# Full-height products, grouped head outputs and line-aligned operands in a two-block transformer kernel

## The chip, the cores and the metric

The kernel runs on one core of a Trainium2 chip as one program of some 24,000 instructions. The metric is the device time of one execution in microseconds (us). The engines are named as in the profile: PE is TensorE's matrix multiply and PEld its weight load, DVE is VectorE, ACT is ScalarE, POOL is GpSimd, SP is SyncE, which here only starts transfers.

## The reference

Two transformer blocks on 512 tokens of width 1024. The first block has a state space branch (a scan in chunks, 8 groups of 4 heads of 64, state 128, 16 extra tokens in front), a short convolution branch, and a retrieval layer that picks experts by top-k; the second block has two kinds of attention and an MLP. What the change touches is the scan:

```
def step(state, inp):
    xc, ac, bc, cc = inp
    acum = jnp.cumsum(ac, axis=1)
    seg = acum[:, :, None] - acum[:, None, :]
    decay = jnp.exp(jnp.where(causal, seg, -jnp.inf))
    cb = jnp.einsum('blgn,bsgn->blsg', cc, bc)
    y_diag = jnp.einsum('blsgr,bsgrp->blgrp', cb[..., None] * decay, xc)
    y_off = jnp.einsum('blgn,bgrpn->blgrp', cc, state) * jnp.exp(acum)[..., None]
    to_end = jnp.exp(acum[:, -1:] - acum)
    new_state = (state * jnp.exp(acum[:, -1])[..., None, None]
                 + jnp.einsum('blgn,blgr,blgrp->bgrpn', bc, to_end, xc))
    return new_state, y_diag + y_off
...
y = group_rmsnorm(y * jax.nn.silu(z), norm_g, SSD_N_GROUPS)
```

The kernel takes chunks of 128 tokens for the 512, and one of 16 in front.

## The kernel before

**Exact products in three parts.** Nearly every large product is float32 made of three products of a shorter float type: `split` (L170) makes a high part `h` on ACT and a low part `l` on DVE or POOL (`wh`, `wl` of a weight tile `wr`; `uh`, `ul` of the input), and `mm3` (L201) issues, for each of 8 slices of depth, high by high, high by low and low by high. The products that use plain float32 (the scan's own) come in the trace as two instructions each, transposes as one. In `A.matmul(out, s, m)` the second operand is held in the array and has up to 128 columns, the third is streamed and has up to 512.

**A projection** loads a 512 KB weight tile on SP's queue into one of 3 buffers (`weights`, L183), splits it (3 buffers for `wh` and `wl`), and runs either 24 products of 512 columns (`mm3_real`, the 512 real tokens) or 48 of 264 or 258 (`mm3_all`, with the tokens in front, in two halves).

**The state space stage** (`ssd_group`, L554, called for 8 groups) has, for each group: projections `BT`, `CT`, `xT0`, `xT1`, each followed by a convolution of four taps and a silu (`conv_silu`: one ACT pass, three DVE passes, a tanh, one DVE pass); the table `cb` of 128 by 128 for each chunk (product `pcb`); for each of 4 heads a product `pb` that spreads the running sum `acum` over the partitions. Its operands `identr` and `acT` have 64 rows: 32 of high parts, 32 of low parts. From `pb` come `E = exp(pb)` on ACT and the decay `W`: on DVE four instructions of 128 columns, `min(pb - acum of the key's token, 0)`, then one exp of 512 columns on ACT, then a product with `cb` on DVE. POOL multiplies `E` by `CT` in place. Then the loop over chunks: transposes into `ptt`, `xdt` and `xe` (DVE), `bt` (ACT), the product `pst`, the new state `st`. For the first chunk `n` is 16, and transposes, `xe`, `bt` and `pst` have 16 rows. Then for j in 0, 1 the projection `z` of 512 columns, and in `py` the heads' outputs: for each of 4 chunks 4 products with 64 held columns, two heads side by side in halves of the array. `ssd_norm` (L656) is a generator: the first `next` makes the sum of squares (`pq`) and the reciprocal root by Newton steps on DVE (`gqx`, `gqa`, `gqy`); the second spreads it with `pr` and multiplies. Of the next group, both `next` calls stand between its projections.

**What sets the order.** The tile framework's scheduler lays each engine's instructions out in a fixed order when the program is built; an engine then takes them strictly in that order. `keep_in_program_order` and `after` (L831, an edge without a wait) pin single instructions. Buffers come from stacks of memory, one from the left and one from the right (`side="right"`); a tile that is not a multiple of 128 bytes moves the start of all that are opened after it on its side. The right-hand stack starts 96 bytes past a multiple of 128.

**The expert stage** (`up`, `second_mm`, L1060) runs 128 expert blocks: products `psu` of 384 columns, and `acc`, 18 products of 512 columns for a block, whose held operand is `ch` or `cl` and whose streamed one is a `pv` weight tile. While it runs, a gather of 128 rows at a time goes on through POOL's queue and DVE.

Of the kernel before, what the change touches and what calls it, by code (L numbers as in the profile page):

```python
# [9 lines left out]
F32 = mybir.dt.float32  # L10
# [12 lines left out]
S = 512  # L23
NM = 16
# [130 lines left out]
class K:  # L155
# [46 lines left out]
    def mm3(self, ps, w, xs, first=True, last=True):  # L202

        kn = len(xs)
        n, tot = 0, 3 * kn
        wh, wl = w
        for k in range(kn):
            xh, xl = xs[k]
            for a, b in ((wh, xh), (wh, xl), (wl, xh)):
                self.nc.tensor.matmul(ps, a[:, k], b, start=first and n == 0, stop=last and n == tot - 1)  # L210
                n += 1

    def mm3_all(self, ps2, w, x, skip=0):

        xh, xl = [a[:, :, skip:] for a in x]
        H = (T - skip) // 2
        for c in range(2):
            self.mm3(ps2[:, 512 - H + c * H:512 + c * H], w,
                     [(xh[:, k, c * H:(c + 1) * H], xl[:, k, c * H:(c + 1) * H]) for k in range(8)])

# [58 lines left out]
    def run(self):  # L279
        nc = self.nc  # L280
        self.cms = {}
        cp = self.open("const")
        self.wraw = self.open("wraw", 3)
        self.whl = self.open("whl", 3)
        self.pt = cp.tile([128, _PN], F32, name="pt")
        self.ct = cp.tile([128, _CN], F32, name="ct")
        self.ones = cp.tile([128, 128], F32, name="ones")
        nc.vector.memset(self.ones, 1.0)

        nc.scalar.activation(self.ones[:, :1], self.ones[:, :1], AF.Copy)  # L290
        nc.scalar.dma_start(self.pt, self.A["par"])
        self.identr = cp.tile([64, 32], F32R, name="identr")
        self.hp = cp.tile([128, 160], F32, name="hp")
        self.res = cp.tile([128, 8, S], F32, name="res")
        self.g12 = cp.tile([128, 8], F32, name="g12")
        self.dpool = self.open("dram", space=DRAM)
        self.sgd = self.dpool.tile([8, 128, S], F32, name="sgd")
        self.gd = self.dpool.tile([16, 128, S], F32, name="gd")
        self.md = self.dpool.tile([16, 128, NC, 128], F32, name="md")
        self.actd = [self.dpool.tile([128, 8, ND], F32, name="actd%d" % g) for g in range(16)]  # L300
        self.mixers()
        self.peer()
        self.block2()
        self.close(*reversed(list(self.cms)))


    def mixers(self):
# [4 lines left out]
        self.u = [up.tile([128, 8, T], F32R, name=n) for n in ("uh", "ul")]  # L312
# [62 lines left out]
        v.tensor_tensor(self.identr, self.cst("ident")[:64, :32], self.cst("ident")[:64, 32:64], op=OP.add)  # L375
# [94 lines left out]
    def proj_real(self, w, i):  # L470
        ps = self.mmtile()[:, :S]
        self.mm3_real(ps, self.weights(self.A[w][i]), self.u)
        return ps
# [15 lines left out]
    def dt_stage(self, dp, p, v):  # L489
# [30 lines left out]
        ahl = dp.tile([64, T], F32R, name="acumhl")  # L520
        nc.scalar.activation(ahl, ac, AF.Copy)
        nc.vector.tensor_tensor(ahl[32:], ac[32:], ahl[32:].bitcast(F32), op=OP.subtract)
# [3 lines left out]
    def dt_tokens(self, dp, srcs):  # L526
# [8 lines left out]
        v4 = pt[:, :480].rearrange("p (c j h) -> p c j h", c=5, j=3)  # L535
        nc.vector.tensor_copy(tok[:NM, 0], v4[:NM, 0])
        nc.vector.tensor_copy(tok[:, 1:], v4[:, 1:])
        self.tok = tok

# [14 lines left out]
    def ssd_group(self, g, yn, sb, s1):  # L554
# [4 lines left out]
        def proj(w, blk, name, skip=0):  # L559
            ps = self.mmtile()  # L560
            self.mm3_all(ps, self.weights(w), self.u, skip)
# [4 lines left out]
        BT = proj(A["w_b"][g], 16 + g, "BT")  # L566
        CT = proj(A["w_c"][g], 24 + g, "CT", SKIP)
# [3 lines left out]
        next(self.fin, None)  # L571
        xT.append(proj(A["w_x"][2 * g + 1], 2 * g + 1, "xT1"))
# [14 lines left out]
        for h in range(4):  # L587
            hh = g * 4 + h
            pb = sp.tile([128, 512], F32, tag="pa", name="pb")
            nc.tensor.matmul(pb, self.identr[:, hh:hh + 1].to_broadcast([64, 128]), acT[:, NM:],  # L590
                             start=True, stop=True)
            nc.scalar.activation(E[:, h], pb, AF.Exp)
            for c in range(4):
                nc.vector.tensor_scalar(W[:, h, c * 128:(c + 1) * 128], pb[:, c * 128:(c + 1) * 128],
                                        tok[:, c + 1, 0, hh:hh + 1], 0.0, op0=OP.subtract, op1=OP.min)
            nc.scalar.activation(W[:, h], W[:, h], AF.Exp)
# [7 lines left out]
        for c, (o, n) in enumerate(self.chunks):  # L604
# [18 lines left out]
            nc.tensor.matmul(pst, bt[:n], xe[:n], start=True, stop=True)  # L623
# [11 lines left out]
        for j in range(2):  # L635
            pz = self.proj_real("w_z", 2 * g + j)
# [3 lines left out]
            py = sp.tile([128, 512], F32, tag="py", name="py")  # L640

            for c in range(4):
                cs = slice(c * 128, (c + 1) * 128)
                for n, (a, b) in enumerate(((xdt[:, c], W), (states[c], Cx))):
                    for h in (2 * j, 2 * j + 1):
                        r = 64 * (h % 2)
                        nc.tensor.matmul(py[r:r + 64, cs], a[:, h * 64:(h + 1) * 64], b[:, h, cs],
                                         start=n == 0, stop=n == 1, skip_group_check=True)
# [418 lines left out]
    def peer_v(self, mm):  # L1067
# [58 lines left out]
        x, y, a = [rp.tile([128, 2, 4], F32, name=n) for n in ("nrx", "nry", "nra")]  # L1126
# [68 lines left out]
    def block2(self):  # L1195
# [14 lines left out]
        sk8 = qp.tile([128, 8], F32, name="sk8")  # L1210
# [94 lines left out]
        eps4 = cn.tile([128, 4], F32, name="eps4")  # L1305
# [322 lines left out]
```

## Time and profile before

| | us |
|---|---|
| median of 3 runs | 2778.41 |
| lowest, highest | 2777.58, 2779.73 |
| the profiled execution | 2778.32 |
| its span, first to last instruction | 2776.6 |
| state space stage, one group (table `cb` to the next table) | 48.70 |

The profile is one execution. A busy share says how much of the time an engine had an instruction in it. A PE product is recorded from its start to the end of its way through the array, so that products overlap in the records; how long it holds the array is read from one start to the next. The granted clock (PEclk) is TensorE's, as a share of 2.4 GHz.

### The profile page before, as it was taken

How to read it: one execution, taken by the hardware profiler on the slowest of the kernel's cores; microseconds unless marked ns; L12 is line 12 of the kernel's file. 1: busy time of each engine (PE TensorE's matmuls, PEld its weight loads, DVE VectorE, ACT ScalarE, POOL GpSimd, SP SyncE). 2: the span in 40 equal slices, each digit the busy share in tenths (PEclk: the TensorE clock that was granted, in tenths of full speed). 3: DMA queues.
4: the chain of work that ended last, by engine and by line, in shares of the span. 5: the costliest groups of instructions: out<-in, count | busy, mean ns of one | idle time of the engine just before them, and what ended most of it. 6: DMA issues, size and time to landing. Idle time of an engine off the chain costs nothing.

```text
span 2776.6 us, 40120 instructions
## 1 busy us (share of the span) xinstructions
PE 2729.3 (98%) x15546; PEld 2366.1 (85%) x15546; DVE 1905.5 (69%) x3707; ACT 1084.8 (39%) x1730; POOL 725.9 (26%) x406
## 2 busy tenths in 40 slices
PE   8999999999999999999999999999999999999998
PEld 8988888887878999999899898877788777988887
DVE  8433777775259999768887777888887766741225
ACT  4323334344233344444333333333344554543232
POOL 2444445443543002000222221222210000144441
PEclk9999999999999999999999999999999999999999
DMA  4222121223342468889988887999952324333232
GB/s 144 92 95 96 62 66 64 69 66 118 114 144 77 138 235 282 262 291 289 366 323 310 318 307 295 384 367 376 375 191 88 96 83 141 129 107 99 91 99 99
DMA packets 173439, 509.96 MB, mean 184 GB/s; under 512 B 14016, under 2 KB 75456, under 8 KB 156736
## 3 DMA queue, kind: packets, MB, share of 16 engines
q1 hardware_dynamic: 89600, 324.42, 34.1%
q0 software_dynamic: 18432, 134.23, 12.5%
q10 hardware_dynamic: 65216, 48.75, 5.5%
q8 instruction: 122, 2.00, 0.3%
q14 instruction: 69, 0.57, 0.1%
HBM read 457.73 MB, written 49.09 MB: 183 GB/s over the span
## 4 chain that ended last, share of the span: by engine, by line
PE 59%; DVE 12%; DMA 4%; ACT 1%; issue 1%; ACTq 0%; SPq 0%; DVEq 0%
PE psu L210 14%; PE acc L1064 14%; PE mmt L210 6%; PE psup L210 6%; PE psdn L210 6%; PE ps L210 4%; DMA wr<-pv 3%; DVE wl L177 2%; PE psw L210 2%; PE po L210 2%; PE pm L1021 1%; ACT wh L176 1%; PE psml L1582 1%; DVE ae L1007 1%; DVE si L713 1%
## 5 line engine op out<-in xcount | busy, mean ns | idle before, releaser
L176 ACT ACTIVATE wh<-wr 128x1024 fp32r<-128x1024 f32 (+1 forms) x503 | 530.6, 1056 | 1083.5 <-issue 225.1
L177 POOL TENSOR_TENSOR wl<-wr,wh 128x1024 fp32r<-128x1024 f32 x180 | 437.2, 2429 | 947.9 <-ACT wh L176 937.5
L177 DVE TENSOR_TENSOR wl<-wr,wh 128x1024 fp32r<-128x1024 f32 (+1 forms) x323 | 391.6, 1213 | 167.9 <-ACT wh L176 165.8
L869 POOL DMA_INDIRECT gb<-puv,idx x128 | 200.8, 1569 | 928.5 <-DVE gacc L877 775.3
L210 PE MATMUL psu<-u2h,wh 128*128 128x384 f32 x1024 | 347.8, 340 | 0.0
L210 PE MATMUL psu<-u2h,wl 128*128 128x384 f32 x1024 | 344.6, 337 | 0.2 <-DVE wl L177 0.2
L210 PE MATMUL psu<-u2l,wh 128*128 128x384 f32 x1024 | 344.0, 336 | 0.0
L210 PE MATMUL mmt<-uh,wh 128*128 128x264 f32 (+2 forms) x1016 | 327.2, 322 | 0.9 <-DVE sc L486 0.9
L210 PE MATMUL mmt<-ul,wh 128*128 128x264 f32 (+2 forms) x1016 | 327.6, 322 | 0.0
L210 PE MATMUL mmt<-uh,wl 128*128 128x264 f32 (+2 forms) x1016 | 325.1, 320 | 0.0
L1064 PE MATMUL acc<-wh,ch 128*128 128x512 f32 x768 | 306.2, 399 | 4.2 <-ACT ch L176 2.2
L1064 PE MATMUL acc<-wl,ch 128*128 128x512 f32 x768 | 305.7, 398 | 1.3 <-DVE wl L177 1.3
L1064 PE MATMUL acc<-wh,cl 128*128 128x512 f32 x768 | 305.9, 398 | 0.1
L210 PEld LDWEIGHTS mmt<-ul,wh 128*128 128x128 f32 x1016 | 191.3, 188 | 21.3 <-issue 10.0
L210 PEld LDWEIGHTS mmt<-uh,wh 128*128 128x128 f32 x1016 | 191.3, 188 | 15.3 <-issue 1.4
L210 PEld LDWEIGHTS mmt<-uh,wl 128*128 128x128 f32 x1016 | 191.5, 188 | 14.8 <-issue 3.3
L210 PEld LDWEIGHTS psu<-u2h,wh 128*128 128x128 f32 x1024 | 193.6, 189 | 2.2
L210 PEld LDWEIGHTS psu<-u2l,wh 128*128 128x128 f32 x1024 | 193.7, 189 | 2.0
L210 PEld LDWEIGHTS psu<-u2h,wl 128*128 128x128 f32 x1024 | 193.3, 189 | 0.6 <-DVE wl L177 0.6
L1064 PEld LDWEIGHTS acc<-wl,ch 128*128 128x128 f32 x768 | 145.5, 189 | 39.0 <-DVE wl L177 3.5
L1064 PEld LDWEIGHTS acc<-wh,ch 128*128 128x128 f32 x768 | 145.2, 189 | 38.2 <-ACT wh L176 2.9
L1064 PEld LDWEIGHTS acc<-wh,cl 128*128 128x128 f32 x768 | 145.3, 189 | 33.4 <-DVE cl L177 0.4
(515 smaller groups left out, 5448.1 us busy)
## 6 DMA issues: line engine op xcount, KB each, us to landing
wr<-pu SPq DMA_DIRECT2D x128, 512.0 KB, 5.5
wr<-pv SPq DMA_DIRECT2D x128, 512.0 KB, 6.1
mg<-md SPq DMA_DIRECT2D x34, 768.0 KB, 10.1
md<-stg ACTq DMA_DIRECT2D x24, 1024.0 KB, 7.7
wr<-w_dn SPq DMA_DIRECT2D x36, 512.0 KB, 3.7
wr<-w_up SPq DMA_DIRECT2D x35, 512.0 KB, 3.7
actd<-at ACTq DMA_DIRECT2D x79, 192.0 KB, 4.0
ag<-actd SPq DMA_DIRECT2D x19, 768.0 KB, 6.8
```

The source lines that it names most:

```text
L176: nc.scalar.activation(h, src, AF.Copy)
L177: (eng or nc.vector).tensor_tensor(l, src, h.bitcast(F32), op=OP.subtract)
L210: self.nc.tensor.matmul(ps, a[:, k], b, start=first and n == 0, stop=last and n == tot - 1)
L713: v.max_index(x[:, 8:16], m[:, 8:16], s2)
L869: keep(nc.gpsimd.indirect_dma_start(out=rows[k][:NG], out_offset=None, in_=self.A["puv"], in_offset=bass.IndirectOffsetOnAxis(ap=idx[:NG, ...
L1007: v.tensor_tensor(pairs(ae), io.rearrange("p (k r) -> p k r", r=2)[:, None].to_broadcast(B4o), w(iT), op=OP.is_equal)
L1021: nc.tensor.matmul(pm[:, t], ae[:, t, 0], B[:, t, j], start=j == 0, stop=j == 1)
L1064: self.nc.tensor.matmul(self.accs[i], a[:, t], b[:, d], start=e == self.e1 and n == 0, stop=e == self.e1 - 1 and n == 2)
L1582: nc.tensor.matmul(ps[:, :N], qh[:, h, bs], kh[:, h, :N], start=True, stop=True)
```

## The change

Six edits.

1. `identr` and `acT` get 128 rows (64 of them zeros) instead of 64, and the first chunk is treated with 128 rows; the rows of `tok` beyond 16 are zeroed.
2. The products of `py` are chained by `after`: of j = 0 none stands ahead of the last `pst`, of j = 1 none ahead of the last product of its `z`.
3. The low parts `wl` of `BT`, `CT` and the two `z` move from POOL to DVE, four of the six in a group (`xT0`, `xT1` stay on POOL).
4. The decay: one DVE instruction of 512 columns takes `min(pb, acum of the key's token)`; the subtraction becomes the bias of the exp, which is now four ACT instructions of 128 columns. The bias is a new tile `ntok`.
5. The second `next(self.fin)`, with `pr`, moves from before `xT1` to the middle of it.
6. Memory: `u`'s rows are 544 floats of which the view takes the last 528, so that the real tokens start at a multiple of 128 bytes in each row; the small tiles `nrx`, `nry`, `nra` (96 bytes together) become one at the bottom of the right-hand stack; `sk8` and `eps4` are padded. By the addresses in the built program: the held `ch`, `cl` of the expert stage and the streamed `ch`, `cl`, `mh`, `ml` go from 96 bytes past a multiple of 128 to 0; `fh`, `fl`, `oh2`, `ol2`, `m2h`, `m2l` (second block) from 64 to 0; the 512 real columns of `uh`, `ul` from 0 or 64, by row, to 0. The halves of 264 and 258 columns stay off.

```diff
+        nr = self.open("nr", side="right").tile([128, 3, 2, 4], F32, name="nr")
+        self.nr = [nr[:, i] for i in range(3)]
...
-        self.u = [up.tile([128, 8, T], F32R, name=n) for n in ("uh", "ul")]
+        self.u = [up.tile([128, 8, 32 + S], F32R, name=n)[:, :, 32 - NM:] for n in ("uh", "ul")]
...
-        ahl = dp.tile([64, T], F32R, name="acumhl")
-        nc.scalar.activation(ahl, ac, AF.Copy)
-        nc.vector.tensor_tensor(ahl[32:], ac[32:], ahl[32:].bitcast(F32), op=OP.subtract)
+        ahl = dp.tile([128, T], F32R, name="acumhl")
+        nc.gpsimd.memset(ahl[64:].bitcast(F32), 0.0)
+        nc.scalar.activation(ahl[:64], ac, AF.Copy)
+        nc.vector.tensor_tensor(ahl[32:64], ac[32:], ahl[32:64].bitcast(F32), op=OP.subtract)
...
+        nc.gpsimd.memset(tok[:, 0], 0.0)
         nc.vector.tensor_copy(tok[:NM, 0], v4[:NM, 0])
         nc.vector.tensor_copy(tok[:, 1:], v4[:, 1:])
         self.tok = tok
+        self.ntok = dp.tile([128, 4, 32], F32, name="ntok")
+        nc.gpsimd.tensor_scalar(self.ntok, tok[:, 1:, 0], -1.0, None, op0=OP.mult)
...
-        BT = proj(A["w_b"][g], 16 + g, "BT")
-        CT = proj(A["w_c"][g], 24 + g, "CT", SKIP)
+        BT = proj(A["w_b"][g], 16 + g, "BT", eng=nc.vector)
+        CT = proj(A["w_c"][g], 24 + g, "CT", SKIP, eng=nc.vector)
 
         next(self.fin, None)
         xT = [proj(A["w_x"][2 * g], 2 * g, "xT0")]
-        next(self.fin, None)
-        xT.append(proj(A["w_x"][2 * g + 1], 2 * g + 1, "xT1"))
+        xT.append(proj(A["w_x"][2 * g + 1], 2 * g + 1, "xT1", mid=lambda: next(self.fin, None)))
...
-            nc.tensor.matmul(pb, self.identr[:, hh:hh + 1].to_broadcast([64, 128]), acT[:, NM:],
+            nc.tensor.matmul(pb, self.identr[:, hh:hh + 1].to_broadcast([128, 128]), acT[:, NM:],
                              start=True, stop=True)
             nc.scalar.activation(E[:, h], pb, AF.Exp)
+            nc.vector.tensor_tensor(W[:, h].rearrange("p (c l) -> p c l", c=4), pb.rearrange("p (c l) -> p c l", c=4),
+                                    tok[:, 1:, 0, hh:hh + 1].to_broadcast([128, 4, 128]), op=OP.min)
             for c in range(4):
-                nc.vector.tensor_scalar(W[:, h, c * 128:(c + 1) * 128], pb[:, c * 128:(c + 1) * 128],
-                                        tok[:, c + 1, 0, hh:hh + 1], 0.0, op0=OP.subtract, op1=OP.min)
-            nc.scalar.activation(W[:, h], W[:, h], AF.Exp)
+                cs = slice(c * 128, (c + 1) * 128)
+                nc.scalar.activation(W[:, h, cs], W[:, h, cs], AF.Exp, bias=self.ntok[:, c, hh:hh + 1])
...
-        for c, (o, n) in enumerate(self.chunks):
+        for c, (o, _) in enumerate(self.chunks):
+            n = 128
...
-            pz = self.proj_real("w_z", 2 * g + j)
+            pz = self.proj_real("w_z", 2 * g + j, nc.vector)
+            prev = self.last_mm if j else last_st
...
-                        nc.tensor.matmul(py[r:r + 64, cs], a[:, h * 64:(h + 1) * 64], b[:, h, cs],
-                                         start=n == 0, stop=n == 1, skip_group_check=True)
+                        o = nc.tensor.matmul(py[r:r + 64, cs], a[:, h * 64:(h + 1) * 64], b[:, h, cs],
+                                             start=n == 0, stop=n == 1, skip_group_check=True)
+                        self.after(o, prev)
+                        prev = o
...
-        x, y, a = [rp.tile([128, 2, 4], F32, name=n) for n in ("nrx", "nry", "nra")]
+        x, y, a = self.nr
...
-        sk8 = qp.tile([128, 8], F32, name="sk8")
+        sk8 = qp.tile([128, 32], F32, name="sk8")[:, :8]
...
-        eps4 = cn.tile([128, 4], F32, name="eps4")
+        eps4 = cn.tile([128, 16], F32, name="eps4")[:, :4]
```

Outside the state space stage the order on every engine stays as it was, but for `ntok` and the zeroing on POOL. Inside it moves. On PE, at the end of the second group's state loop, before (`mmt` is a projection's product, here the next group's `BT` and `CT`):

```order
L647 MATMUL py_3042<-W_2897,xdt_2943 64x128 x2
L647 MATMUL py_3042<-E_2896,st3_2999 64x128 x2
L210 MATMUL mmt_3116<-uh_98,wh_3119 128x264
L210 MATMUL mmt_3116<-ul_99,wh_3119 128x264
L210 MATMUL mmt_3116<-uh_98,wl_3120 128x264
L210 MATMUL mmt_3116<-uh_98,wh_3119 128x264
L210 MATMUL mmt_3116<-ul_99,wh_3119 128x264
L210 MATMUL mmt_3116<-uh_98,wl_3120 128x264
L210 MATMUL mmt_3180<-uh_98,wh_3183 128x258
L210 MATMUL mmt_3180<-ul_99,wh_3183 128x258
L647 MATMUL py_3042<-W_2897,xdt_2943 64x128 x2
```

and on PE at the same place now:

```order
L638 MATMUL pst_3005<-xe_3003,btok_3001 128x256
L622 MATMUL ptt_3012<-ct_65,xT0_2817 128x128
L622 MATMUL ptt_3012<-ct_65,xT1_2888 128x128
L664 MATMUL py_3050<-W_2905,xdt_2951 64x128 x2
L664 MATMUL py_3050<-E_2904,st0_2962 64x128 x2
L664 MATMUL py_3050<-W_2905,xdt_2951 64x128 x2
L664 MATMUL py_3050<-E_2904,st1_2975 64x128 x2
L664 MATMUL py_3050<-W_2905,xdt_2951 64x128 x2
L664 MATMUL py_3050<-E_2904,st2_2991 64x128 x2
L664 MATMUL py_3050<-W_2905,xdt_2951 64x128 x2
L664 MATMUL py_3050<-E_2904,st3_3007 64x128 x2
```

The four chunks of j = 0 were spread singly among the projections; now they stand in one run behind the last transposes. Over the stage there were 40 runs of `py` products and there are 16.

On DVE, between the second group's table `cb` and the first chunk's `xe`, before (`cacc` and `xT` are the convolution of `xT1`):

```order
L580 TENSOR_TENSOR cb<-pcb,ct 128x512
L549 SCALAR_TENSOR_TENSOR cacc<-mmt,hp,cacc 128x527
L549 SCALAR_TENSOR_TENSOR cacc<-mmt,hp,cacc 128x526
L594 TENSOR_SCALAR W<-pb,tok 128x128
L549 SCALAR_TENSOR_TENSOR cacc<-mmt,hp,cacc 128x525
L594 TENSOR_SCALAR W<-pb,tok 128x128 x3
L552 SCALAR_TENSOR_TENSOR xT_2880<-ctanh,cacc 128x528
L597 TENSOR_TENSOR W<-W,cb 128x512
L594 TENSOR_SCALAR W<-pb,tok 128x128 x4
L620 TENSOR_TENSOR xe<-ptt,tok 16x256
```

and on DVE now, right behind `cb`:

```order
L177 TENSOR_TENSOR wl<-wr,wh 128x1024
L561 SCALAR_TENSOR_TENSOR cacc<-mmt,hp,cacc 128x527
L606 TENSOR_TENSOR W<-pb,tok 128x512
L561 SCALAR_TENSOR_TENSOR cacc<-mmt,hp,cacc 128x526
L561 SCALAR_TENSOR_TENSOR cacc<-mmt,hp,cacc 128x525
L611 TENSOR_TENSOR W<-W,cb 128x512
L606 TENSOR_TENSOR W<-pb,tok 128x512
L564 SCALAR_TENSOR_TENSOR xT_2888<-ctanh,cacc 128x528
L177 TENSOR_TENSOR wl<-wr,wh 128x1024
L611 TENSOR_TENSOR W<-W,cb 128x512
L606 TENSOR_TENSOR W<-pb,tok 128x512
L635 TENSOR_TENSOR xe<-ptt,tok 128x256
```

Two `wl` and the heads' second and third `W` now stand ahead of `xe`, whose product `pst` waits for it. On PE that `pst` moved too, from the 30th to the 40th projection product behind `pcb`.

On PE around `pr`, second group's norm among the third group's projections, before (3269 is `xT0`, 3340 `xT1`):

```order
L210 MATMUL mmt_3269<-uh_98,wh_3272 128x264
L210 MATMUL mmt_3269<-ul_99,wh_3272 128x264
L210 MATMUL mmt_3269<-uh_98,wl_3273 128x264
L258 MATMUL pr_3333<-ct_65,gqy_3255 128x128 x4
L210 MATMUL mmt_3340<-uh_98,wh_3343 128x264
L210 MATMUL mmt_3340<-ul_99,wh_3343 128x264
L210 MATMUL mmt_3340<-uh_98,wl_3344 128x264
```

and on PE there now (3341 is `xT1`):

```order
L210 MATMUL mmt_3341<-uh_102,wh_3344 128x264
L210 MATMUL mmt_3341<-ul_103,wh_3344 128x264
L210 MATMUL mmt_3341<-uh_102,wl_3345 128x264
L260 MATMUL pr_3372<-ct_65,gqy_3263 128x128 x4
L210 MATMUL mmt_3341<-uh_102,wh_3344 128x264
L210 MATMUL mmt_3341<-ul_103,wh_3344 128x264
L210 MATMUL mmt_3341<-uh_102,wl_3345 128x264
```

`pr` now has 24 more products of 264 columns ahead of it.

## Rows read from the trace of the kernel before

**Rows 1.** The page's first part: busy us, share of the span, instructions, by engine.
```profile
PE 2729.3 (98%) x15546; PEld 2366.1 (85%) x15546; DVE 1905.5 (69%) x3707; ACT 1084.8 (39%) x1730; POOL 725.9 (26%) x406
```
**Rows 2.** Windows, one group: stretch, length, busy us (count), clock, DMA share, GB/s.
```profile
319.40:368.10 48.70, 48.27 (x353) 41.15 (x352) 35.44 (x79) 19.32 (x30) 21.86 (x15) 1.00 0.21 67
```
**Rows 3.** Timeline of PE around a 64-row product: start us, us, line, out<-in, shape.
```profile
272.45 0.40 PE L210 MATMUL mmt<-uh,wh 128*128 128x512 f32 x1
...
273.54 0.39 PE L210 MATMUL mmt<-uh,wl 128*128 128x512 f32 x1
```
**Rows 4.** Timeline of PE around the 16-row product of the first chunk.
```profile
280.24 0.49 PE L210 MATMUL mmt<-ul,wh 128*128 128x512 f32 x1
...
281.59 0.48 PE L210 MATMUL mmt<-uh,wl 128*128 128x512 f32 x1
```
**Rows 5.** Timeline of PE around the same products of a later chunk, with 128 rows.
```profile
291.12 0.28 PE L210 MATMUL mmt<-ul,wh 128*128 128x264 f32 x1
...
291.92 0.37 PE L210 MATMUL mmt<-uh,wl 128*128 128x264 f32 x1
```
**Rows 6.** Timeline of PE: one chunk of head outputs between projection products.
```profile
293.22 0.28 PE L210 MATMUL mmt<-uh,wh 128*128 128x264 f32 x1
...
294.24 0.28 PE L210 MATMUL mmt<-uh,wl 128*128 128x264 f32 x1
```
**Rows 7.** Timeline of PE: four chunks of head outputs in one run.
```profile
298.09 0.28 PE L210 MATMUL mmt<-ul,wh 128*128 128x258 f32 x1
...
300.42 0.28 PE L210 MATMUL mmt<-uh,wh 128*128 128x258 f32 x1
```
**Rows 8.** Timeline of PE at the spreading of the norm: in brackets idle time, releaser.
```profile
312.42 0.28 PE L210 MATMUL mmt<-uh,wl 128*128 128x264 f32 x1
313.03 0.65 PE L258 MATMUL pr<-ct,gqy 128*128 128x128 f32 x4 [0.32 <-DVE gqy L253]
```
**Rows 9.** Windows, projections of 512 columns whose operands all start at multiples of 128.
```profile
700.00:740.00 40.00, 40.00 (x178) 33.12 (x177) 2.75 (x4) 0.00 (x0) 1.00 0.37 116
```
**Rows 10.** Windows, L1064: one block's 18 products, held operand 96 past.
```profile
1500.26:1504.47 4.21, 4.21 (x18) 3.20 (x18) 1.00 0.92 346
```
**Rows 11.** Windows, 512 columns: streamed `mh`, `ml` 96 past.
```profile
775.00:800.00 25.00, 25.00 (x109) 20.12 (x108) 3.34 (x5) 0.00 (x0) 1.00 0.50 151
```
**Rows 12.** Windows, 512 columns: streamed `fh`, `fl` 64 past.
```profile
2500.00:2540.00 40.00, 40.00 (x176) 32.81 (x176) 1.00 0.31 99
```
**Rows 13.** Windows: streamed `uh`, `ul`, 512 columns, eight products, 0 or 64 past.
```profile
274.69:276.32 1.63, 1.63 (x8) 1.31 (x7) 1.00 0.58 161
```
**Rows 14.** Windows, 256 columns: sixteen aligned products.
```profile
2445.01:2446.93 1.92, 1.92 (x18) 1.92 (x17) 0.42 (x1) 0.36 (x1) 1.00 0.59 228
```
**Rows 15.** Windows, 256 columns: 20 us with streamed operands 64 past.
```profile
2360.00:2380.00 20.00, 20.00 (x171) 20.00 (x169) 2.61 (x7) 1.00 0.69 215
```
**Rows 16.** Timeline of DVE from the table `cb` to the first chunk's `xe`.
```profile
320.47 0.69 DVE L580 TENSOR_TENSOR cb<-pcb,ct 128x512 f32<-128x512 f32 x1 [1.04 <-PE pcb L577]
...
327.71 0.40 DVE L620 TENSOR_TENSOR xe<-ptt,tok 16x256 f32<-16x256 f32 x1
```
**Rows 17.** Groups of one group's stretch on DVE: line, out<-in, shapes, count, busy us, mean ns.
```profile
L594 DVE TENSOR_SCALAR W<-pb,tok 128x128 f32<-128x128 f32 x16 | 4.6, 340 | 0.7 <-ACT E L592 0.7
L597 DVE TENSOR_TENSOR W<-W,cb 128x512 f32<-128x512 f32 x4 | 4.0, 988 | 0.4 <-ACT W L596 0.4
```
**Rows 18.** The same view on ACT.
```profile
L596 ACT ACTIVATE W<-W 128x512 f32<-128x512 f32 x4 | 2.5, 630 | 3.7 <-DVE W L594 3.6
...
L618 ACT ACTIVATE btok<-ptt 128x128 f32<-128x128 f32 x3 | 0.8, 275 | 3.7 <-DVE xdt L613 3.7
```
**Rows 19.** The page's fifth part: the low parts on DVE.
```profile
L177 DVE TENSOR_TENSOR wl<-wr,wh 128x1024 fp32r<-128x1024 f32 (+1 forms) x323 | 391.6, 1213 | 167.9 <-ACT wh L176 165.8
```
**Rows 20.** Windows, expert stage: PE, PEld, DVE, ACT, POOL, clock, DMA share, GB/s.
```profile
1750.00:1800.00 50.00, 50.00 (x216) 40.17 (x215) 43.14 (x66) 18.00 (x32) 13.09 (x9) 1.00 1.00 400
1900.00:1950.00 50.00, 48.15 (x199) 38.01 (x198) 41.91 (x64) 18.57 (x32) 11.54 (x8) 0.97 0.93 360
```

More of the change, by code (lines that the diff above doesn't have):

```diff
@@ L209, in mm3, with mm3_all @@
             for a, b in ((wh, xh), (wh, xl), (wl, xh)):
-                self.nc.tensor.matmul(ps, a[:, k], b, start=first and n == 0, stop=last and n == tot - 1)
+                self.last_mm = self.nc.tensor.matmul(ps, a[:, k], b, start=first and n == 0, stop=last and n == tot - 1)
                 n += 1
-    def mm3_all(self, ps2, w, x, skip=0):
+    def mm3_all(self, ps2, w, x, skip=0, mid=None):
         xh, xl = [a[:, :, skip:] for a in x]
@@ L219, in mm3_all @@
                      [(xh[:, k, c * H:(c + 1) * H], xl[:, k, c * H:(c + 1) * H]) for k in range(8)])
+            if mid and c == 0:
+                mid()
     def mm3_real(self, ps, w, x, off=NM, n=S):
@@ L291, in run @@
         nc.scalar.dma_start(self.pt, self.A["par"])
-        self.identr = cp.tile([64, 32], F32R, name="identr")
+        self.identr = cp.tile([128, 32], F32R, name="identr")
         self.hp = cp.tile([128, 160], F32, name="hp")
@@ L373, in mixers @@
         sc.append(self.sc_in(sct, 1, d, rb2))
-        v.tensor_tensor(self.identr, self.cst("ident")[:64, :32], self.cst("ident")[:64, 32:64], op=OP.add)
+        v.tensor_tensor(self.identr, self.cst("ident")[:, :32], self.cst("ident")[:, 32:64], op=OP.add)
         o = _POFF["conv_w"][0]
@@ L468, in proj_all, with proj_real @@
         return ps
-    def proj_real(self, w, i):
+    def proj_real(self, w, i, eng=None):
         ps = self.mmtile()[:, :S]
-        self.mm3_real(ps, self.weights(self.A[w][i]), self.u)
+        self.mm3_real(ps, self.weights(self.A[w][i], eng=eng), self.u)
         return ps
@@ L557, in ssd_group, with proj @@
         tok, acT = self.tok, self.acT
-        def proj(w, blk, name, skip=0):
+        def proj(w, blk, name, skip=0, eng=None, mid=None):
             ps = self.mmtile()
-            self.mm3_all(ps, self.weights(w), self.u, skip)
+            self.mm3_all(ps, self.weights(w, eng=eng), self.u, skip, mid)
             o = sb.tile([128, T - skip], F32, tag=name, name=name)
@@ L622, in ssd_group @@
             pst = sp.tile([128, 256], F32, tag="ps", name="pst")
-            nc.tensor.matmul(pst, bt[:n], xe[:n], start=True, stop=True)
+            last_st = nc.tensor.matmul(pst, bt[:n], xe[:n], start=True, stop=True)
             new = s1.tile([128, 256], F32, tag="st%d" % c, name="st%d" % c)
```

## Prediction

> **What bounds the kernel now.** I read the page's first part first: PE is busy for 2729.3 of 2776.6 us, and no other engine passes 69% [rows 1]. That is an average, so next I took the windows view over one group of the state space stage, where most of the change lies: in 48.70 us PE is busy for 48.27, DVE for 35.44, POOL for 21.86, ACT for 19.32, and the granted clock is 1.00 (the 2.4 GHz level) [rows 2]. PE sets the pace there, and DVE has 13 us to spare. A busy PE can still be slow, since records of products overlap. So the third reading is PE's timeline from one start to the next around each kind of product that the change touches [rows 3 to 8], and the fourth the rate of plain projection products by where their operands start [rows 9 to 15]. What the change is worth is what it takes off these starts, less what it makes PE wait for.
>
> **The change part by part.** The sum is made against the profiled execution, 2778.32 us; its span is 2776.6, so 1.7 lie around it. The median of the runs is 2778.41, the same within 0.1.
>
> *The measure: one aligned product of 512 columns.* A window counts products that reach in over its edge: a record lasts 0.39 us [rows 3] and starts come every 0.23, so 1.7 are taken off. With all operands at multiples of 128 bytes that gives 40.00 / (178 − 1.7) = 0.2269 us [rows 9].
>
> *A. `pb` with 128 rows.* From the projection product ahead of a `pb` to the one after the next pass 1.09 us [rows 3]; in it start three products of 512 columns: two of `u` and `pb`. At the 0.2329 of `u`'s products (E below) that would be 0.70. So the 64-row product costs 0.39 us beyond its columns, half at its start, half at the start of what follows. If full height takes this away, 4 × 8 = 32 products give 32 × 0.39 = 12.5 us.
>
> *B. The first chunk with 128 rows.* A projection product, `pst` and the next chunk's three transposes take 1.35 us where `pst` has 16 rows [rows 4], and 0.80 where it has 128, with a projection product of 264 columns (0.12) in place of one of 512 (0.23) [rows 5]; like with like that is 0.80 − 0.12 + 0.23 = 0.91. Eight groups give 8 × 0.44 = 3.5 us. Zeroed rows of `tok` keep the sums the same.
>
> *C. `py` in runs.* One chunk alone takes 1.02 us less two products of 264 columns, 0.78 [rows 6]; four chunks in one run take 2.33 − 0.24 = 2.09, or 0.52 for each [rows 7]. So entering and leaving the half-width products costs about 0.35 us. Per group there were 4 × 0.78 + 2.09 = 5.21 us, and will be 2 × 2.09 = 4.18: 8 × 1.03 = 8.2 us. The chain holds `py` of j = 0 back behind the last transposes; its readers on DVE have all of the second `z` left, so I cost that at nothing, hidden by PE's projections.
>
> *D. `pr` later.* `pr` starts 0.61 us after a product of 264 columns, with 0.32 idle on `gqy` [rows 8]; 0.61 − 0.12 = 0.49, in seven of the eight groups (the last has no projections around it): 3.4 us. Half of `xT1`'s products, 24 × 0.12 = 2.9 us, now lie ahead of it, well over the 0.32. Some 0.1 of the 0.49 may be the products' own start; I take it all.
>
> *E. Alignment.* By one subtraction for each kind: the expert stage's `acc` takes 4.21 / 18 = 0.2339 [rows 10], so 0.0070 over the aligned product, times 128 × 18 = 2304 products: 16.1 us. The projections streaming `mh` or `ch`: 25.00 / 107.3 = 0.2330 [rows 11], 0.0061 × 384 = 2.3. Those streaming `fh` or `oh2`: 40.00 / 174.3 = 0.2295 [rows 12], 0.0026 × 768 = 2.0. Those streaming the 512 real columns of `uh`: 1.63 / 7 = 0.2329 (seven starts; the eighth record reaches in) [rows 13], 0.0060 × 936 = 5.6, of which 384 products are the `z`. Against it, 256 columns take 1.92 / 16 = 0.120 aligned (two of the 18 reach over the edges) [rows 14] and 20.00 / 169 = 0.118 when 64 past [rows 15]; 576 products give about 1 back. The sum is 25.0 us. No row shows the same product in both places, so that the address makes the difference is inferred from which kinds are slow.
>
> Two rules speak against parts of this. The Trainium skill, "TensorE: Matmul & The Clock Gate", section "Back-to-back issue gap", gives the gap of an isolated product from its columns and the clock alone, and "SBUF — State Buffer", section "Operand start alignment", tells of legality, not of speed. By them E is worth nothing and the time is that of the first rival below; this trace doesn't agree so far, since its rows differ by 3% at equal columns and clock. The first of these pages of the Trainium skill, section "Why this matters for your kernels", says that one product with 32 rows takes the time of one with 128. By that A and B are worth nothing, which is the second rival; [rows 3] and [rows 4] show a price where the height changes.
>
> *F. What is given back in the stage.* From `cb` to the first chunk's `xe` DVE takes 7.24 us [rows 16]. On this way now stand three instructions of 512 columns instead of eight of 128 (4.6 / 16 each, 2.3) [rows 17], one more product with `cb` (0.99), and two `wl` of 1.21 [rows 19]. The minimum of 512 columns is not in the trace; its bounds are `cb` (0.69, also PSUM in) [rows 16] and the product (0.99) [rows 17]. I take 0.69, the row with the same kind of operand: 2.1 − 2.3 + 1.0 + 2.4 = 3.2 us later. On PE `pst` stands ten projection products later, 2.3 us, less three times the 0.39 of A: 1.1 later. So `pst` may wait for up to 2.1 us. But DVE's way of 7.24 us held waits for PE and ACT, so much of this is slack: 0 to 0.9 us per group by that, 0 to 7 in the stage. I take 2. ACT has 16 exps of 128 columns, bounded by `btok` with 128 (0.275), for four of 630 ns [rows 18]: 4.4 − 2.5 = 1.9 us more on an engine with 29 to spare. DVE in all: 35.4 − 4.6 + 4 × 0.69 to 0.99 + 4 × 1.21 is 38.4 to 39.6 in a period of 48.70 − 27.6 / 8 = 45.2: still 6 us free. POOL loses four `wl`. `ntok` and the zeroing run once, beside projections, at nothing.
>
> *G. What is given back in the expert stage.* There the DMA engines are busy for 1.00 and 0.93 of the time, and in the second stretch PE stood for 1.85 of 50 us and the clock fell to 0.97 [rows 20]: transfers already arrive last in places. A faster `acc` asks for its tiles earlier. If it holds for two thirds of the 128 blocks (my choice, from two stretches seen), 0.0070 × 18 × 83 = 10.5 us of the 16.1 of E is at stake; at worst all. I take 6.
>
> Sum: 12.5 + 3.5 + 8.2 + 3.4 + 25.0 = 52.6 us gained, 2 + 6 given back: 44.6. 2778.3 − 44.6 is 2733.7, **2734 us**.
>
> **Rivals.**
> *Alignment does nothing.* The slow kinds could be slow for something else (what shares the memory, the held operand). For it: no row shows the address alone changing. The rule behind it is that of the Trainium skill, in the two sections named under E. Against it: four kinds, each slower where its operand is off. Then 2778.3 − 27.6 + 2 = **2753**.
> *Height does nothing by itself.* The 0.39 around `pb` could be the broadcast held operand or a change of data type, which stay. [Rows 4] against [rows 5] speaks against it, with the same operands and only the height different, but that comparison rests on two places. The rule behind it is that of the Trainium skill, "TensorE: Matmul & The Clock Gate", section "Why this matters for your kernels". Then A and B fall away: 2734 + 16 = **2750**.
> *The expert stage is held by its transfers.* If all of `acc`'s gain is given back, the sum loses 10 more: **2744**. For it: 1.00 busy at 400 GB/s [rows 20]. Against it: PE is busy in all of those 50 us.
> *The stage's gain is taken by waits.* With 2.5 to 3.2 us more of waits in each group, and alignment worth nothing, it gives 2778.3 − 27.6 + 20 to 26 = 2771 to 2777; I put it at 2776, **no change**.
> *Slower: DVE becomes the bound of the state space stage.* If the minimum of 512 columns with an operand spread over columns cost 2.5 us instead of 0.69, and `pst`, `ptt` and the `z` had to wait in turn, DVE would need 35.4 − 4.6 + 10 + 4.8 = 45.6 busy; with the gaps of its dependent chain (13 in 48.70 before) the period could rise to 52. It decides from a period above 48.70 + (25 / 8) = 51.8 with E whole. At 52.5: 2778.3 + 8 × 3.8 − 25 = **2783**, E whole. Against it: DVE's instructions of this size take 0.7 to 1.2 us everywhere in these rows.
>
> **How the numbers follow.** The forecast, 2734, has 0.60; its own range, 2722 (nothing given back, 2726, and 4 us for the unknown costs) to 2743 (7 and 10 given back). Alignment does nothing 0.14, expert stage held 0.14, height does nothing 0.05, no change 0.04, slower 0.03. The range runs from 2722 to 2756, over the first four cases; left out are the last two and tails of the others, some 0.2. A measurement of this kernel can tell about 0.2%, 5.6 us, from no change: faster 0.94, same 0.03, slower 0.03.
>
> **What would show it.** A and B: three products around `pb` in 0.70 us, and the first chunk's stretch in 0.91. C: 16 runs of `py` of 2.1 us. D: no idle at `pr` in seven groups. All of it: a group in about 45 us. E: 18 products of `acc` in 4.08 us, `z` at 0.2269. F: idle of PE ahead of `pst`, released by `xe`, in each group. G: PE idle and a lower clock between 1700 and 2050 us. The forecast is wrong if `acc` stays at 4.21 us for a block, if `pb` keeps its 0.39, or if a group stays above 47 us.

## The result, and the profile after

| | before, us | changed, us |
|---|---|---|
| median (4 runs each) | 2778.83 | 2749.74 |
| lowest, highest | 2777.58, 2779.73 | 2746.01, 2752.14 |
| the profiled execution | 2778.32 | 2746.01 |
| its span | 2776.6 | 2744.2 |

The ratio is 0.9897, with a 95% interval of 0.9885 to 0.991: faster by 29 us, where 44.6 were forecast. The time, 2749.7, lies in the range (2722 to 2756) and 15.7 above the forecast. It is nearest to the 2750 of the rival in which height does nothing and the 2753 of the one in which alignment does nothing, but neither is what happened, as the rows show. Single runs differ by some microseconds (in the later comparisons the kernel before took 2772.99 to 2782.88), and the profiled run of the changed kernel is its fastest, so the account below is made for that execution.

The order of PE is the same in both programs outside the stage, so the same product can be looked up in both traces. Its start, in us from the start of the span, and before less after:

| product | before | after | gained by then |
|---|---|---|---|
| first table `cb` (`pcb`) | 270.75 | 269.63 | 1.1 |
| last group's table | 611.16 | 588.97 | 22.2 |
| first projection of `yh`, behind the stage | 681.88 | 660.48 | 21.4 |
| first `psu` | 923.59 | 901.09 | 22.5 |
| last `psu` | 1710.09 | 1680.35 | 29.7 |
| last `acc` | 2068.51 | 2035.95 | 32.6 |
| last product's end | 2767.68 | 2735.37 | 32.3 |

Up to the end of the stage 21.4 were gained where 31.2 were forecast (27.6 of A to D, the 5.6 of `u`, less 2); the expert stage gave 10 between the first `psu` and the last `acc`, as forecast (16.1 less 6).

The page's first part and the window of one group answer to [rows 1] and [rows 2]; the window's columns are stretch, length, busy us (count) of PE, PEld, DVE, ACT, POOL, clock, DMA share, GB/s:

```profile
PE 2693.1 (98%) x15546; PEld 2370.3 (86%) x15546; DVE 1901.0 (69%) x3643; ACT 1102.6 (40%) x1826; POOL 644.4 (23%) x377
```
```profile
315.23:360.84 45.61, 45.45 (x353) 41.59 (x352) 34.62 (x71) 21.57 (x42) 12.48 (x11) 1.00 0.22 70
```

A group takes 45.6 us (48.6 before; 45.2 forecast). POOL has gone from 21.9 to 12.5 busy, and DVE, which got four `wl` of 1.22 us more, did not rise at all: 34.62, where 38.4 to 39.6 were forecast. That is the first surprise. PE's timeline around a `pb`, a run of `py`, and a block of `acc` (its first product, and the `psu` behind its last) answers to [rows 3], [rows 7] and [rows 10]:

```profile
325.89 0.39 PE L210 MATMUL mmt<-uh,wh 128*128 128x512 f32 x1
326.11 0.40 PE L210 MATMUL mmt<-ul,wh 128*128 128x512 f32 x1
326.35 0.40 PE L602 MATMUL pb<-acumhl,identr 128*128 128x512 f32 x1
326.59 0.39 PE L210 MATMUL mmt<-uh,wl 128*128 128x512 f32 x1
...
340.91 0.28 PE L210 MATMUL mmt<-uh,wl 128*128 128x258 f32 x1
...
343.25 0.28 PE L210 MATMUL mmt<-ul,wh 128*128 128x258 f32 x1
...
1398.10 0.39 PE L1083 MATMUL acc<-wh,ch 128*128 128x512 f32 x1
...
1402.22 0.33 PE L210 MATMUL psu<-u2h,wh 128*128 128x384 f32 x1
```

Three products around `pb` take 0.70 us (1.09 before). A run of four chunks takes 343.25 − 340.91 = 2.34, as before, and all 16 runs are such. The 18 products of a block of `acc` take 4.12, 0.2289 each (4.21 and 0.2339 before). But the products of `u` stayed slow, at 0.2322 on the mean of their starts behind the stage (0.2319 before).

### The profile page after: what moved, and what is told of

It reads as the page before. It is cut to its first block, busy times and chain, and to the rows that moved or that the text cites. A ratio compares the mean times of both kernels' runs of the same rounds, so it can differ in the third digit from the quotient of the medians.

```text
span 2744.2 us, 40146 instructions
## 1 busy us (share of the span) xinstructions
PE 2693.1 (98%) x15546; PEld 2370.3 (86%) x15546; DVE 1901.0 (69%) x3643; ACT 1102.6 (40%) x1826; POOL 644.4 (23%) x377
## 4 chain that ended last, share of the span: by engine, by line
PE 57%; DVE 13%; DMA 5%; ACT 1%; issue 1%; POOL 0%; ACTq 0%; SPq 0%; DVEq 0%; POOLq 0%
PE psu L210 14%; PE acc L1083 11%; PE psdn L210 6%; PE mmt L210 6%; PE psup L210 6%; DMA wr<-pv 4%; PE ps L210 4%; DVE wl L177 3%; PE psw L210 2%; PE po L210 2%; PE pm L1040 1%; ACT wh L176 1%; DVE gb L916 1%; PE psml L1601 1%; DVE ae L1026 1%
## 5 line engine op out<-in xcount | busy, mean ns | idle before, releaser
L177 POOL TENSOR_TENSOR wl<-wr,wh 128x1024 fp32r<-128x1024 f32 x148 | 360.2, 2434 | 850.5 <-ACT wh L176 826.4
L177 DVE TENSOR_TENSOR wl<-wr,wh 128x1024 fp32r<-128x1024 f32 (+1 forms) x355 | 430.7, 1214 | 174.3 <-ACT wh L176 167.7
L888 POOL DMA_INDIRECT gb<-puv,idx x128 | 192.8, 1507 | 926.9 <-DVE gacc L896 769.5
```

The source lines that it names most:

```text
L177: (eng or nc.vector).tensor_tensor(l, src, h.bitcast(F32), op=OP.subtract)
L888: keep(nc.gpsimd.indirect_dma_start(out=rows[k][:NG], out_offset=None, in_=self.A["puv"], in_offset=bass.IndirectOffsetOnAxis(ap=idx[:NG, ...
```

## Experiments

All times are medians; the kernel before had 2777 to 2779 in each comparison.

**What makes 512 columns fast.** In the changed kernel every streamed operand starts at a multiple of 128 bytes, and yet `u` stayed slow while `acc`, `mh`, `fh` became fast. By the addresses in the built program, all fast kinds start at 128 past a multiple of 256 in both operands; `u`'s rows, 2176 bytes apart, alternate between 0 and 128. Three kernels move one of them (in the first two the squares at the start also have 2 buffers for 3).

```diff
 # u_phase128 (and u_phase0, with 32 - NM:32 + S)
-up.tile([128, 8, 32 + S], F32R, name=n)[:, :, 32 - NM:]
+up.tile([128, 8, 64 + S], F32R, name=n)[:, :, 64 - NM:]
 # right_shift128
-nr = ... .tile([128, 3, 2, 4], F32, name="nr")
+nr = ... .tile([128, 56], F32, name="nr")[:, :24].rearrange("p (i t a) -> p i t a", i=3, t=2)
```

> The changed kernel, but u's rows are 576 floats apart and the real tokens of every row start 128 bytes past a multiple of 256, as the held weights do (in the changed kernel the rows alternate between 0 and 128 past). To make room the squares at the start have 2 buffers for 3. Theory P (what counts is that the streamed and the held operand start at the same place in a line of 256 bytes): the 936 products of u with 512 columns go from 0.233 to 0.227 us, some 5 us less than the changed kernel. Theory Q (a multiple of 128 is enough, u is slow for something else): they stay at 0.233, no change of time.

> The same as u_phase128, but the real tokens of every row start at a multiple of 256, 128 bytes off the held weights. Theory P: the products of u stay at 0.232 to 0.235 us, and the kernel is some 5 us slower than u_phase128. A theory R (only the change of place from row to row is slow, any constant place is fast): 0.227 here too. Theory Q: 0.233, no difference from u_phase128.

> The changed kernel with 128 bytes more in the small tile at the bottom of the right-hand stack: the held ch and cl of the expert stage and the streamed ch, cl, mh, ml are still at multiples of 128 bytes, but 128 off the other operand within 256. Theory P: acc goes back to 0.234 us for a product (0.227 in the changed kernel), the projections of ch and mh to 0.232, so 0.007 x 2304 + 0.005 x 384 = 18 us at most are lost, 8 to 18 with what the expert stage's transfers take. Theory Q: acc stays at 0.227, no change of time.

Measured: u_phase128 2744.99 (2743.51 to 2747.01), u_phase0 2750.56 (2746.44 to 2752.19), 5.6 apart, right_shift128 2753.55 (2752.12 to 2756.95). The windows over a stretch of nothing but `u`'s products, of the changed kernel, u_phase128 and u_phase0; then PE's timeline of a block of `acc` in right_shift128:

```profile
628.00:660.00 32.00, 32.00 (x139) 25.84 (x138) 23.23 (x23) 16.21 (x27) 14.27 (x6) 1.00 0.46 135
```
```profile
625.00:656.00 31.00, 31.00 (x138) 25.67 (x137) 22.96 (x23) 16.01 (x26) 14.02 (x6) 1.00 0.45 138
```
```profile
629.00:661.00 32.00, 32.00 (x140) 25.95 (x139) 23.08 (x23) 16.10 (x27) 14.13 (x6) 1.00 0.45 134
```
```profile
1400.45 0.39 PE L1083 MATMUL acc<-wh,ch 128*128 128x512 f32 x1
...
1404.62 0.34 PE L210 MATMUL psu<-u2h,wh 128*128 128x384 f32 x1
```

A count in a window of 32 us is good to one product, so the rates are better read from the starts themselves, over 142 steps in a row: a product of `u` takes 0.2322 us in the changed kernel, 0.2270 at constant 128 past, 0.2323 at constant 0. A block of `acc`, held operand moved by 128, takes 4.18 us, 0.2320 for a product, against 4.12 and 0.2289 (0.234 had been expected). So a multiple of 128 is not enough and theory Q falls, and R falls with u_phase0, whose place is constant. Where all rows of an operand start at one place, theory P holds: the two operands have to start at the same place within 256 bytes. The price of a miss by 128 is 0.003 to 0.005 us of 0.227. What P alone does not explain is the changed kernel's `u`: half of its rows do start at the place of the held operand, and yet in no slice does a product come near 0.227 (the means of three products go through 0.235, 0.231, 0.232 and 0.231 in turn, over and over). Rows that alternate are as slow as a constant miss; why, no run here shows. That right_shift128 lost only 3.8 us of the 8 to 18 belongs to the next question.

**Where `acc`'s gain went.**

```diff
 # before_right: the kernel before with nr, sk8, eps4 of edit 6 and nothing else
 # half_before, half_right: the kernel before and before_right with
-out=rows[k][:NG], ... / r = rows.pop(k)[:NG, 1024:]
+out=rows[k][:NG, :1024], ... / r = rows.pop(k)[:NG, :1024]
 # and the table that they gather from keeps only its first half
```

> The kernel before, with the right-hand part of edit 6 alone (the small tiles at the bottom of the right-hand stack, sk8 and eps4 padded; u's rows as before). acc at 0.227, the projections of ch and mh at 0.227, those of fh at 0.227, and 256 columns at 0.120 for 0.116. By the products' rates 0.007 x 2304 + 0.006 x 384 + 0.0025 x 768 - 0.0045 x 570 = 17.8 us are gained. If the expert stage's transfers give part of it back, as in the changed kernel (stalls of acc on wh every 70 us or so), 8 to 13 us are left; if nothing of it is given back, 17 or more.

> The kernel before, but the gather beside the expert stage brings 4 KB for each row instead of 8 (the second half is left out and the first used in its place, so this part of the output is another). It is the base for half_right. If the stalls of acc in this kernel (5.5 us in all) come from transfers, most of them go: 2772 to 2777 us. If not: 2778.

> before_right with the same halved gather. By the products' rates alignment on the right is worth 15.2 us (acc 14.4 to 15.2, ch and mh 2.3, fh and oh2 1.8, less 3.3 at 256 columns), of which before_right kept 7.5. Theory T (the transfers of the expert stage took the rest): it is 13 to 16 us below half_before, and the stalls of acc, 9.2 us in before_right, fall under 3. Theory S (something else took it, such as the supply by ACT and DVE, or the clock): again 7 to 9 below half_before, with the stalls still there.

Measured: before_right 2771.22, ratio 0.9974 (0.9964 to 0.9983), 7.5 us; half_before 2769.25, below the 2772 to 2777 expected; half_right 2751.44. With half the gather the same edit is worth 17.8 us, 2 above theory T's range. The windows from 1720 to 2000 us, where PE does nothing but `acc`, of the kernel before, before_right, half_before and half_right, in this order:

```profile
1720.00:2000.00 280.00, 277.88 (x1177) 222.13 (x1176) 245.89 (x376) 99.69 (x175) 67.59 (x44) 0.99 0.96 375
```
```profile
1720.00:2000.00 280.00, 272.65 (x1178) 221.50 (x1177) 243.51 (x370) 100.15 (x174) 67.73 (x45) 0.99 0.96 380
```
```profile
1720.00:2000.00 280.00, 280.00 (x1197) 225.11 (x1196) 252.03 (x386) 101.91 (x178) 75.35 (x46) 1.00 0.84 305
```
```profile
1720.00:2000.00 280.00, 280.00 (x1237) 231.83 (x1236) 260.04 (x396) 105.96 (x186) 78.99 (x48) 1.00 0.86 311
```

PE got through as many products in these 280 us with either alignment: the faster one only stood idle for 7.3 us instead of 2.1. With the traffic down by some 18% the counts are 1197 and 1237. A fixed window makes it look a little worse than it is, since the faster kernel is further on in its work: from the last `psu` to the last `acc` the same 1494 products took 358.4 and 354.4 us with the whole gather, 351.8 and 340.5 with half of it. So alignment kept 4.0 of 11.3 us there; the transfers took the rest, and theory T holds.

**Each edit of the stage alone, and one undone.**

```diff
 # before_rows: the kernel before with edit 1
 # before_py: the kernel before with edit 2
 # rows_dve: the kernel before with edits 1, 3 and 4
 # wl_pool: the changed kernel, edit 3 undone
-BT = proj(A["w_b"][g], 16 + g, "BT", eng=nc.vector)
+BT = proj(A["w_b"][g], 16 + g, "BT")
```

> The kernel before with edit 1 alone (pb and the first chunk with 128 rows). As predicted: 12.5 + 3.5 = 16 us less, three products around a pb in 0.70 us, the first chunk's pst and transposes 0.44 us shorter. The rival, that height does nothing by itself: no difference. A gain in between if the product of 128 rows waits for xe or keeps a part of the price.

> The kernel before with edit 2 alone, py in 16 runs. As predicted 8.2 us less in the groups; the last group gives 1 to 3 back through its norm (as read in the changed kernel), so 5 to 7 less in all. If DVE's last steps of a group (y, then the norm) come too late for the next group's products: less than 3.

> The kernel before with edits 1, 3 and 4 (full height, four wl per group on DVE, the shorter decay). Edit 1 alone gave 5.8 us of the 16 expected; PE then waited 0.88 us at a pb in each group for DVE to free the buffer of the pb ahead. If the slow W on DVE (1.88 us while POOL makes a wl, 0.68 otherwise) is what held that buffer, the three edits together give 16 to 19: the whole of edit 1, and up to 3 for the waits at pb and pr in the kernel before. If edits 3 and 4 are worth at most the 4.1 us that PE was idle in the stage before: 6 to 10.

> The changed kernel with edit 3 undone: all six wl of a group on POOL again. If DVE's longer way is what PE waits for at the first transposes of a group (0.17 us idle, 0.34 us in all, in each of eight groups) and behind xe, 2 to 3 us are gained. If instead the wl of the projections come too late from POOL (2.43 us each there, 1.21 on DVE), PE waits in front of projections, and it is slower by 2 us or more.

Measured: before_rows 2771.32 (ratio 0.9977, 0.9968 to 0.9987), 5.8 us and not 16; before_py 2784.23 (1.0019, 1.0009 to 1.0029), slower by 5.8; rows_dve 2774.51 (0.9985, 0.9975 to 0.9994), 3.9 and below both expectations; wl_pool 2758.83, 9 slower than the changed kernel, where 2 to 3 gained or waits in front of projections had been expected. What PE waited for in the stage, in the view of waits (us in total, times, longest), of the four in this order:

```profile
PE pb L592 <- DVE W L596: 7.0, 8, 0.9
```
```profile
PE pst L623 <- DVE xe L620: 11.9, 8, 1.5
```
```profile
PE pq L229 <- POOL q L667: 8.1, 8, 2.3
PE ptt L613 <- DVE xT L556: 1.3, 7, 0.2
```
```profile
PE pb L602 <- DVE W L606: 6.6, 8, 0.8
PE mmt L210 <- DVE gqy L255: 2.8, 7, 0.4
```

The prices of PE's products moved as predicted in each of them (the stretch that a `pb` adds is 0.24 for 0.63 us; the `py` of before_py sum to 33.5 for 41.8), but each gain opened a wait of its own: for the buffer of `pb`, for `xe`, for `q`. In the kernel before PE waited in the stage for `gqy` (2.3 us in all) and once for `q` (0.9), for nothing else: its slow products had covered DVE's chain. In wl_pool none of the waits is for a `wl`, so it isn't that the slower POOL delivers them too late. DVE's and POOL's timelines in wl_pool show why that chain is slow there:

```profile
326.02 1.83 DVE L611 TENSOR_TENSOR W<-W,cb 128x512 f32<-128x512 f32 x1
327.77 0.68 DVE L606 TENSOR_TENSOR W<-pb,tok 128x512 f32<-128x512 f32 x1
```
```profile
324.90 2.40 POOL L177 TENSOR_TENSOR wl<-wr,wh 128x1024 fp32r<-128x1024 f32 x1
```

`W` times `cb` takes 1.83 us and ends half a us after POOL's `wl`; alone it takes 0.68 (four per group in the changed kernel):

```profile
L177 DVE TENSOR_TENSOR wl<-wr,wh 128x1024 fp32r<-128x1024 f32 x4 | 4.9, 1219 | 1.1 <-ACT wh L176 1.1
...
L611 DVE TENSOR_TENSOR W<-W,cb 128x512 f32<-128x512 f32 x4 | 2.7, 683 | 1.0 <-ACT W L610 1.0
L606 DVE TENSOR_TENSOR W<-pb,tok 128x512 f32<-128x512 f32 x4 | 2.7, 682 | 0.0
```

The 0.988 of [rows 17] was a mean of two kinds: of the 32 such instructions in the kernel before, the eight that overlap a `wl` on POOL took 1.88 us, the 24 others 0.69. So a `wl` on POOL cost DVE 1.2 us where it met such an instruction (in before_py, where 16 of them met one, up to 2.47 us for one instruction), and four `wl` of 1.22 moved to DVE raised its busy time in a group by only 1.3 us in sum, from 33.3 in wl_pool to 34.6. The Trainium skill, "SBUF — State Buffer", section "Who interferes with whom", has this rule: an instruction of DVE with two inputs in SBUF contends with one of GpSimd that reads SBUF, the pair of ports that they share is locked by one of them at a time, and the order of issue decides who blocks. These rows agree with it (the `wl` had started 1.1 us ahead of the `W`); I had not weighed it.

**A better version.** Two more kernels on top of u_phase128:

```diff
 # u128_chain
-                        self.after(o, prev)
+                        if g < 7:
+                            self.after(o, prev)
 # u128_chain_gather, in addition
-FIRST, FUSED = 0.25, 1.3
+FIRST, FUSED = 0.25, 1.6
```

> u_phase128 without the chain of py in the last group. The chain there holds the last head outputs behind the last z with nothing of a next group to hide it: PE waits 2.3 us for pq instead of 0.9 in the kernel before, and six products behind it run at the half clock (0.43 us for 0.23). If the chain is the cause: 1 to 2.7 us less than u_phase128 (a run of single chunks costs 1 back). If the last norm waits for something else: no difference.

> u128_chain with the gather asking for 1.6 rows of 128 per expert block instead of 1.3 in the first half of the expert stage, so that fewer are left for the second half, where the DMA engines were busy for 0.96 of the time and acc stalled for some 8 us. If the second half's transfers alone hold acc there, the stalls go and 4 to 8 us are gained. If the first half then lacks transfers or DVE time, stalls move there: no gain, or a loss.

Measured: u128_chain 2744.46 (2742.01 to 2749.67), no difference from u_phase128; PE still waits 2.2 us for `pq` (2.3 in the changed kernel). So the chain isn't the cause of that wait. In the changed kernel's trace POOL's `q` of the last group stands right behind a `wl`:

```profile
617.19 2.38 POOL L177 TENSOR_TENSOR wl<-wr,wh 128x1024 fp32r<-128x1024 f32 x1 [8.12 <-ACT wh L176]
619.53 1.44 POOL L680 TENSOR_TENSOR q<-q 128x512 f32<-128x512 f32 x1
...
621.02 1.21 PE L231 MATMUL pq<-ones,q 128*128 128x1 f32 x8 [2.27 <-POOL q L680]
```

Putting that `wl` elsewhere wasn't tried. u128_chain_gather took 2730.56 (2727.45 to 2732.1), ratio 0.9827 (0.9809 to 0.9846): 48 us below the kernel before, 14 below u128_chain, where 4 to 8 had been expected. u128_chain's window in the first half of the expert stage, then those of this kernel in the first and the second:

```profile
1350.00:1650.00 300.00, 300.00 (x1518) 273.04 (x1517) 239.20 (x334) 113.73 (x192) 71.70 (x48) 1.00 0.85 320
```
```profile
1350.00:1650.00 300.00, 299.26 (x1512) 271.64 (x1512) 265.68 (x381) 112.24 (x202) 95.64 (x60) 1.00 0.94 360
1700.00:2000.00 300.00, 300.00 (x1325) 248.43 (x1324) 250.55 (x375) 112.54 (x186) 57.61 (x35) 1.00 0.90 342
```

In the second half PE does its products without a stop, with the whole gather: from the last `psu` to the last `acc` it takes 340.5 us, as half_right does, and 359.5 in u128_chain, whose profiled run was its slowest. The first half, at a DMA share of 0.85 in u128_chain, had room for it. This version beats both kernels.

## Why the prediction was right or wrong, point by point

The direction and the bound (PE's time from start to start) held. The stated range held only because it reached to 2756 to take in the rivals: the forecast's own, 2722 to 2743, was missed by 7. The sum was 12.3 too high against the profiled execution (44.6 forecast, 32.3 measured), and the median lies another 3.7 above that execution.

- **A and B** held as prices: a `pb` adds 0.24 us instead of 0.63, 32 × 0.39 = 12.4 (12.5 forecast); the first chunk's stretch is 0.91 for 1.35, as forecast (3.5). But that stretch begins right behind a `pb`, and 0.11 of it was already in A: 0.9 stood twice in the sum, which leaves 2.6. And the stretches of the second and third chunk rose by 0.12 and 0.06, about 1.5 back, for which the sum had no term. The rival on height falls.
- **C** held: the runs of `py` sum to 33.4 us for 41.8, 8.4 (8.2). "I cost that at nothing, hidden by PE's projections" held in the company of the other edits: alone, edit 2 loses 5.8. That it was edits 3 and 4 that made the difference is argued from DVE's lines; edit 2 with these two alone wasn't tried.
- **D** held: no idle at `pr`, 0.44 for 0.98 us, 3.7 (3.4).
- **E** was the step that failed. "With all operands at multiples of 128 bytes" named the wrong condition. `acc` (4.12 us for a block, 4.08 forecast), `mh`, `ch`, `fh` gained because they came to the same place within 256 bytes as the other operand. `u` didn't, and its 5.6 were missing altogether; [rows 13] held the hint, since half of those products already started at a multiple of 128 and were no faster. The loss at 256 columns was 0.0045 × 570 = 2.6 and not 1.
- **F** had the right size in the groups and the wrong place. Not `pst` but the first transposes wait, for `xT`: 0.34 us in each group, 2.7 in all. Of the terms the minimum was right, 0.682 (0.69 taken); ACT's exps took 0.39 (0.275 taken), the product with `cb` 0.68 (0.99 taken), and DVE's sum missed what POOL's `wl` had cost it. The last group wasn't costed: 1.4 us more of waiting for `pq`, and six products behind it at 0.43 us from start to start for 0.23, the 1.2 GHz level, another 1.3. The granted clock from the last table to the fourth product behind its `pr` is 0.96, and 0.50 over five of the six products (1.00 around `pq` before); these two windows, then two of the products:

```profile
588.97:627.73 38.76, 35.72 (x211) 28.44 (x210) 24.56 (x55) 16.93 (x37) 17.78 (x13) 0.96 0.24 68
```
```profile
622.67:624.80 2.13, 2.13 (x7) 1.65 (x5) 1.62 (x10) 0.00 (x0) 0.00 (x0) 0.50 0.36 140
```
```profile
622.67 0.63 PE L210 MATMUL mmt<-uh,wh 128*128 128x512 f32 x1
623.09 0.63 PE L210 MATMUL mmt<-ul,wh 128*128 128x512 f32 x1
```

- **G** held, mechanism and size, in the profiled execution: the waits of `acc` for the parts of its weights grew from 3.3 to 7.3 us, and about 7 of the gain were given back (6 forecast). That transfers are behind it is shown by half_right and u128_chain_gather. Where the slower runs, up to 2752, lost their time no trace shows. The first `acc` may be a part of it (see the sum below).
- **The slower rival** (DVE becomes the stage's bound) didn't come true, but before_py shows how near it was: with PE's products out of the way `pst` waited 11.9 us for `xe`. Its cause there was not a slow minimum but `W` times `cb` behind POOL: 2.33 to 2.47 us for eight of the 16 that met a `wl`.

With these terms the profiled gain is 25.6 (A to D), 15.4 (E: for `acc` 45 blocks beside `psu` at 4.21 − 4.12 = 0.09, and 83 blocks of 18 at 0.0066, the means of all its starts being 0.2343 and 0.2277, together 13.9; 2.3 and 1.8; less 2.6), less 2.7, 2.7 and 7: 28.6 of 32.3. Of the rest, 1.3 is a shorter wait at the first `acc` (0.9 for 2.2 us) and 1.4 is what came after it: the first block took 6.12 us before, at a granted clock of 0.72, its products coming every 0.43, and 4.58 in the changed kernel, at 1.00.

```profile
1330.35:1336.47 6.12, 6.02 (x18) 4.58 (x19) 5.96 (x10) 2.51 (x6) 1.68 (x1) 0.72 1.01 392
```
```profile
1306.26:1310.84 4.58, 4.48 (x18) 3.49 (x19) 4.54 (x7) 1.48 (x3) 1.23 (x1) 1.00 1.01 418
```

No term of the sum foresaw this 2.7. That wait changes from kernel to kernel (0.9 in right_shift128, 2.8 in u_phase128, 2.4 in u_phase0), and the profiled run is the fastest of four: I call it luck. I can't place the last 1.0.

## What to carry to other kernels

A gain read from an engine's own time is safe only as far as the next chain behind it: edit 1 alone gave a third, edit 2 alone lost, and the edit that seemed to cost (more work on DVE) was worth 9 us, since it paid for the others. Where a stage's transfers are busy for 0.95 of the time, count on less than half of what its products gain until the traffic is moved (4.0 of 11.3 us in before_right); here moving it gave 14 us, more than any edit of the products in that stage. And when a group of kinds is called fast for a property, look for a kind that has the property and is slow before pricing it.

## What the runs showed of the hardware

A product of 512 columns with 4-byte operands takes 0.227 us where all rows of the held and of the streamed operand start at the same place in 256 bytes. It took 0.229 with the streamed one 64 past a multiple of 128 (`fh` before), 0.232 where the two are 128 apart (u_phase0, right_shift128) or where the rows alternate (the changed kernel's `u`), and 0.233 to 0.234 with one of them 96 past (`mh`, `ch` and `acc` before); a common multiple of 128 alone doesn't do it. At 256 columns it is the other way round: 0.115 to 0.116 with one of them 64 past, 0.120 aligned (means of the differences of starts over 190 products of each of three kinds). The Trainium skill, "SBUF — State Buffer", section "Operand start alignment", is on legality and not speed; no run here shows which part of the chip is behind the difference.
